# Issuing the stores of a memory-bound kernel from ScalarE's queue, loads from SyncE's

## Chip, cores, metric

The kernel runs on one core of a Trainium2 chip. The metric is the device time of one execution in microseconds (us). A profiled execution spans about 1.8 us less than its device time (81.2 of 83.02 us before). SP in the profile is SyncE, DVE is VectorE, ACT is ScalarE, and "SPq" and "ACTq" are their queues of transfers.

## The reference

```python
x = np.random.randn(1024, 4096).astype(np.float32)      # axis = -1
mean = np.mean(x, axis=axis, keepdims=True)
return ((x - mean) ** 2).astype(np.float32)
```

16.78 MB are read and 16.78 MB are written.

## The kernel before

The 1024 rows are two tiles of 128 partitions x 4 rows, so one partition's part of a tile is 64 KB in one piece. Both tiles have a buffer of their own, and all loads are issued at once. ScalarE computes the mean of row 3 and most of the squares, VectorE the other means and the last 1792 columns of row 2.

```python
Q = 4; HEAD = 512; H = D * 9 // 16
io = ctx.enter_context(tc.tile_pool(name="io", bufs=ntiles))      # ntiles = 2
for i in range(ntiles):
    x_tile = io.tile([P, Q * D], F32)
    cuts = [0, HEAD, Q * D] if i == 0 else [0, Q * D]
    for lo, hi in zip(cuts, cuts[1:]):
        nc.sync.dma_start(out=x_tile[:, lo:hi], in_=x_t[i][:, lo:hi])
    ...
for i in range(ntiles):
    row = [tiles[i][:, q * D:(q + 1) * D] for q in range(Q)]
    ...                                     # means, squares of rows 3, 0, 1
    square_on_act(row[2][:, :H], m2)
    back = row[2][:, H:]
    nc.vector.tensor_scalar_add(out=back, in0=back, scalar1=m2)
    nc.vector.tensor_mul(out=back, in0=back, in1=back)
    nc.sync.dma_start(out=out_t[i], in_=tiles[i])
```

Of the kernel before, what the change touches and what calls it, by code (L numbers as in the profile page):

```python
# [2 lines left out]

os.environ.setdefault("NEURON_RT_ULTRASERVER_MODE", "4")

# [4 lines left out]

F32 = mybir.dt.float32
ACT = mybir.ActivationFunctionType


@with_exitstack
def kernel(
    ctx: ExitStack,
    tc: tile.TileContext,
    x: bass.AP,
    axis: bass.AP,  # L20
    out: bass.AP,
):




    nc = tc.nc

    B, D = x.shape
    P = nc.NUM_PARTITIONS  # L30
    Q = 4
    HEAD = 512
    H = D * 9 // 16
    assert B % (P * Q) == 0
    ntiles = B // (P * Q)
    inv_d = 1.0 / float(D)

    x_t = x.rearrange("(n p q) d -> n p (q d)", p=P, q=Q)
    out_t = out.rearrange("(n p q) d -> n p (q d)", p=P, q=Q)

    io = ctx.enter_context(tc.tile_pool(name="io", bufs=ntiles))
    scratch = ctx.enter_context(tc.tile_pool(name="scratch", bufs=1))
    stats = ctx.enter_context(tc.tile_pool(name="stats", bufs=2 * ntiles * Q))

    tiles = []
# [5 lines that stand above are left out]
        tiles.append(x_tile)  # L51

    inorder = tc.keep_in_program_order

    def mean_on_act(row):
        copy = scratch.tile([P, D], F32)
        neg_mean = stats.tile([P, 1], F32)
        nc.scalar.activation(  # L58
            out=copy, in_=row, func=ACT.Identity, scale=-inv_d, accum_out=neg_mean
        )  # L60
        return neg_mean

    def mean_on_dve(row):
        neg_sum = stats.tile([P, 1], F32)
        neg_mean = stats.tile([P, 1], F32)
        inorder(nc.vector.reduce_sum(  # L66
            out=neg_sum, in_=row, axis=mybir.AxisListType.X, negate=True
        ))
        inorder(nc.vector.tensor_scalar_mul(out=neg_mean, in0=neg_sum, scalar1=inv_d))  # L69
        return neg_mean  # L70

    def square_on_act(part, neg_mean):
        inorder(nc.scalar.activation(  # L73
            out=part, in_=part, func=ACT.Square, bias=neg_mean, scale=1.0
        ))

    for i in range(ntiles):
        row = [tiles[i][:, q * D:(q + 1) * D] for q in range(Q)]
        m3 = mean_on_act(row[3])
        m0 = mean_on_dve(row[0])  # L80
        square_on_act(row[3], m3)
        m1 = mean_on_dve(row[1])
        square_on_act(row[0], m0)
        m2 = mean_on_dve(row[2])
        square_on_act(row[1], m1)
        square_on_act(row[2][:, :H], m2)
        back = row[2][:, H:]
        nc.vector.tensor_scalar_add(out=back, in0=back, scalar1=m2)  # L88
        nc.vector.tensor_mul(out=back, in0=back, in1=back)  # L89
        nc.sync.dma_start(out=out_t[i], in_=tiles[i])  # L90


# [1 line left out]
_INS = ['x', 'axis']  # L94
_OUTS = [((1024, 4096), 'float32')]

_NUMBERS = {'axis': -1}


# [26 lines left out]
```

## Time and profile before

| | before |
|---|---|
| time, median of 6 runs (range) | 83.06 us (83.00 to 83.20) |
| span of the profiled execution | 81.2 us |
| first store issued / second store issued | 39.42 / 58.70 us |
| last load packets end / first store's last packets end | 41.08 to 41.38 / 60.40 to 60.70 us |

A *packet* is here one record of one transfer engine: in these transfers one partition's row of a tile, 64 KB. A window of the profile (columns: window, width, busy time of DVE, ACT and POOL, clock, DMA share, GB/s) books a packet's whole time where the packet starts. So if a window holds the starts of exactly one packet for each of the 16 engines, its DMA share times its width is the mean duration of those packets. Three windows of the kernel before (columns: window, width, busy time of DVE, ACT and POOL, clock, DMA share, GB/s):

```profile
38.50:39.20 0.70, 0.70 (x1) 0.65 (x1) 0.00 (x0) 1.00 3.47 1498
...
41.00:41.80 0.80, 0.06 (x1) 0.06 (x1) 0.00 (x0) 1.00 3.03 1311
...
60.30:61.80 1.50, 0.00 (x0) 0.00 (x0) 0.00 (x0) 1.00 1.62 699
```

They hold the load's last packets (3.47 x 0.70 = 2.43 us), the first store's first packets (3.03 x 0.80 = 2.42 us) and the second store's first packets (1.62 x 1.50 = 2.43 us). All are alike. Going from the load to the store, and from the store to the next, costs an engine nothing here, on one queue: paired in order of time, each packet starts within 0.01 us of the end of the one before.

### The profile page before, as it was taken

How to read it: one execution, taken by the hardware profiler on the slowest of the kernel's cores; microseconds unless marked ns; L12 is line 12 of the kernel's file. 1: busy time of each engine (PE TensorE's matmuls, PEld its weight loads, DVE VectorE, ACT ScalarE, POOL GpSimd, SP SyncE). 2: the span in 40 equal slices, each digit the busy share in tenths (PEclk: the TensorE clock that was granted, in tenths of full speed). 3: DMA queues.
4: the chain of work that ended last, by engine and by line, in shares of the span. 5: the costliest groups of instructions: out<-in, count | busy, mean ns of one | idle time of the engine just before them, and what ended most of it. 6: DMA issues, size and time to landing. Idle time of an engine off the chain costs nothing.

```text
span 81.2 us, 83 instructions
## 1 busy us (share of the span) xinstructions
DVE 33.4 (41%) x16; ACT 34.7 (43%) x13; POOL 0.2 (0%) x4
## 2 busy tenths in 40 slices
DVE  0000000000099999999349999999800000000000
ACT  6000000000099999999249999999800000000000
POOL 0000000000000000000000000000000000000000
DMA  1999569999974999990999990999992899997490
GB/s 16 614 501 501 219 282 501 501 501 501 517 323 194 517 517 517 517 484 32 517 517 517 517 517 0 517 517 517 517 517 129 388 517 517 517 517 323 194 517 0
DMA packets 720, 33.55 MB, mean 413 GB/s; under 512 B 80, under 2 KB 80, under 8 KB 208
## 3 DMA queue, kind: packets, MB, share of 16 engines
q1 hardware_dynamic: 720, 33.55, 96.2%
HBM read 16.78 MB, written 16.78 MB: 413 GB/s over the span
## 4 chain that ended last, share of the span: by engine, by line
DMA 49%; DVE 21%; SPq 1%; issue 0%
DMA x_tile<-in_x_dram 49%; DVE neg_sum L66 16%; DVE x_tile L89 2%; DVE x_tile L88 1%; SPq L50 1%; DVE neg_mean L69 1%
## 5 line engine op out<-in xcount | busy, mean ns | idle before, releaser
L66 DVE TENSOR_REDUCE neg_sum<-x_tile 128x1 f32<-128x4096 f32 x6 | 26.5, 4413 | 24.9 <-DMA x_tile<-in_x_dram 24.9
L73 ACT ACTIVATE x_tile<-x_tile,neg_mean 128x4096 f32<-128x4096 f32 (+1 forms) x8 | 26.0, 3324 | 0.1
L58 ACT ACTIVATE copy<-x_tile 128x4096 f32<-128x4096 f32 x2 | 7.2, 3616 | 23.0 <-DMA x_tile<-in_x_dram 23.0
L89 DVE TENSOR_TENSOR x_tile<-x_tile 128x1792 f32<-128x1792 f32 x2 | 4.1, 2026 | 0.1
L88 DVE TENSOR_SCALAR x_tile<-x_tile,neg_mean 128x1792 f32<-128x1792 f32 x2 | 2.3, 1153 | 0.1
L58 ACT ACT_TABLE_LOAD x1 | 1.3, 1283 | 0.7 <-PEq L107 0.7
L69 DVE TENSOR_SCALAR neg_mean<-neg_sum 128x1 f32<-128x1 f32 x6 | 0.9, 154 | 0.2
L58 ACT ACTIVATION_READ_ACCUMULATOR copy<-x_tile 128x1 f32 x2 | 0.4, 186 | 0.0
L107 POOL MEMSET const-bfloat16-1.0<- 128x1 bf16 x1 | 0.1, 103 | 0.0
L107 POOL MEMSET const-uint8-127<- 128x1 uint8 x1 | 0.1, 103 | 0.0
L107 POOL MEMSET const-float32-1.0<- 128x1 f32 x1 | 0.1, 100 | 0.0
L107 POOL MEMSET const-float32-0.0<- 128x1 f32 x1 | 0.1, 99 | 0.2 <-issue 0.2
## 6 DMA issues: line engine op xcount, KB each, us to landing
x_tile<-in_x_dram SPq DMA_DIRECT2D x1, 7936.0 KB, 21.2
x_tile<-in_x_dram SPq DMA_DIRECT2D x1, 256.0 KB, 2.7
out_dram<-x_tile SPq DMA_DIRECT2D x2, 21.7
x_tile<-in_x_dram SPq DMA_DIRECT2D x1, 40.1
```

The source lines that it names most:

```text
L50: nc.sync.dma_start(out=x_tile[:, lo:hi], in_=x_t[i][:, lo:hi])
L58: nc.scalar.activation(out=copy, in_=row, func=ACT.Identity, scale=-inv_d, accum_out=neg_mean)
L66: inorder(nc.vector.reduce_sum(out=neg_sum, in_=row, axis=mybir.AxisListType.X, negate=True))
L69: inorder(nc.vector.tensor_scalar_mul(out=neg_mean, in0=neg_sum, scalar1=inv_d))
L73: inorder(nc.scalar.activation(out=part, in_=part, func=ACT.Square, bias=neg_mean, scale=1.0))
L88: nc.vector.tensor_scalar_add(out=back, in0=back, scalar1=m2)
L89: nc.vector.tensor_mul(out=back, in0=back, in1=back)
L107: nc = _bacc.Bacc("TRN2", target_bir_lowering=False, num_devices=1)
```

## The change

The intent is to give loads and stores separate queues, so that a store's wait for its data cannot hold up a load. In the kernel before, no load stands behind a store: SP's load issues end at 2.06 us, and its first store is issued at 39.42 us.

```diff
         nc.vector.tensor_mul(out=back, in0=back, in1=back)
-        nc.sync.dma_start(out=out_t[i], in_=tiles[i])
+        nc.scalar.dma_start(out=out_t[i], in_=tiles[i])
```

## The prediction

> **What bounds the kernel now.** I began with the busy shares, the slices and the queue of the page, because 33.55 MB pass through in about 80 us and the first question is whether the transfers leave room for anything else.
>
> ```profile
> DVE 33.4 (41%) x16; ACT 34.7 (43%) x13; POOL 0.2 (0%) x4
> ...
> DMA  1999569999974999990999990999992899997490
> GB/s 16 614 501 501 219 282 501 501 501 501 517 323 194 517 517 517 517 484 32 517 517 517 517 517 0 517 517 517 517 517 129 388 517 517 517 517 323 194 517 0
> ...
> q1 hardware_dynamic: 720, 33.55, 96.2%
> ```
>
> No compute engine is busy for half of the span, and the one DMA queue is busy for 96.2% of what 16 engines could give. The dips in the DMA row (a 0, a 2, a 4) look like holes. Whether they are holes decides this case, so I cut narrow windows about them; the last two columns are the DMA share and GB/s.
>
> ```profile
> 1.70:1.80 0.10, 0.00 (x0) 0.10 (x1) 0.00 (x0) 1.00 0.98 123
> ...
> 38.60:39.00 0.40, 0.40 (x1) 0.40 (x1) 0.00 (x0) 1.00 6.07 2621
> 39.00:41.00 2.00, 0.36 (x1) 0.15 (x1) 0.00 (x0) 1.00 0.00 0
> 41.00:41.40 0.40, 0.00 (x0) 0.00 (x0) 0.00 (x0) 1.00 6.07 2622
> ...
> 57.90:58.30 0.40, 0.40 (x1) 0.40 (x1) 0.00 (x0) 1.00 6.04 2621
> 58.30:60.30 2.00, 0.33 (x1) 0.20 (x1) 0.00 (x0) 1.00 0.00 0
> 60.30:60.80 0.50, 0.00 (x0) 0.00 (x0) 0.00 (x0) 1.00 4.85 2097
> ...
> 77.20:77.70 0.50, 0.00 (x0) 0.00 (x0) 0.00 (x0) 1.00 4.84 2097
> 77.70:79.60 1.90, 0.00 (x0) 0.00 (x0) 0.00 (x0) 1.00 0.00 0
> ```
>
> A share of 6.07 of 16 engines in 0.4 us is possible only if a packet's whole time is booked where it starts: 6.07 x 0.40 = 2.43 us and 4.85 x 0.50 = 2.42 us for each engine. So each engine starts one packet there that runs for 2.42 us, and the empty window after it is that packet in flight. The packet records agree: a tile's row of 65,536 bytes is one packet of 2.418 us, eight to an engine and transfer, and each starts within 0.02 us of the end of the one before. The dips are bookkeeping and there is no hole. 65,536 B / 2.418 us is 27.1 GB/s for one engine, 434 GB/s for 16, and 33.55 MB at that rate take 77.4 us. The first packets start at 1.75, the last ones at 77.2 to 77.7 and run until about 80.1: 78.3 us without a pause, of which 77.4 is bytes at full rate and 0.9 the start with its small first load. Before it lies 1.75 us of start, after it 1.1 us of landing and closing (span 81.2). The time of 83.02 is 1.8 us above the span, for what lies outside it.
>
> Then the timeline and SP's waits, to see what a later or earlier store would do.
>
> ```profile
> 37.33 2.03 DVE L89 TENSOR_TENSOR x_tile<-x_tile 128x1792 f32<-128x1792 f32 x1
> 39.42 19.62 SPq L90 DMA_DIRECT2D out_dram<-x_tile  x2
> 41.74 3.62 ACT L58 ACTIVATE copy<-x_tile 128x4096 f32<-128x4096 f32 x1 [2.59 <-DMA x_tile<-in_x_dram]
> ...
> 45.48 13.01 ACT L73 ACTIVATE x_tile<-x_tile,neg_mean 128x4096 f32<-128x4096 f32 x4
> ...
> 56.60 2.03 DVE L89 TENSOR_TENSOR x_tile<-x_tile 128x1792 f32<-128x1792 f32 x1
> ```
> ```profile
> SPq L90 <- DVE x_tile L89: 54.7, 2, 35.9
> SPq L121 <- DMA out_dram<-x_tile: 21.2, 2, 19.2
> ```
>
> SP is idle except for issuing: it waits for VectorE's last multiply before each store, then for the stores. No load stands behind a store on SP, since all three loads were issued by 2.1 us. The first store is issued at 39.42; the merged row gives the second at 39.42 + 19.62 - 0.34 = 58.70 (one issue is 0.34 to 0.35 us). From an issue to its first packet I take 1.0 us, from the first load (issued 0.73, first packet 1.75).
>
> So the first store is ready at 40.4, while the loads' last packets, started at 38.6 to 39.0, end at 41.0 to 41.4: it is early by 0.6 to 1.0 us. The second is ready at 59.7, while the first store's last packets, started at 57.9 to 58.3, end at 60.3 to 60.7: early by 0.6 to 1.0 us. The chain of waits gives 21% to VectorE and 49% to the load, but it is a chain through tile 1's computation with hardly any slack against the queue: the transfer queue is what sets the end.
>
> [...]
>
> **The change part by part.** The listing of both programs shows exactly one difference: two issues leave SP's end, and one stands on ScalarE after each tile's 2304-wide activation, with the same waits on ScalarE's and VectorE's semaphores. VectorE's order is the same.
> Removed: 2 x 0.345 = 0.69 us of SP, which is idle then; worth 0 on the path.
> Added: 2 x 0.345 us (SP's duration taken for ScalarE's) on ScalarE. The first sits in ScalarE's idle stretch: its square ends at about 39.15, VectorE at 39.36, so the issue runs from about 39.4 to 39.8, and the next activation waits for the load until 41.74. Margin 1.9 us, cost 0. The second comes after ScalarE's last activation (45.48 + 13.01 = 58.49), again after VectorE's end at 58.63. Cost 0.
> Moved: the issue itself by perhaps 0.05 us either way; it is early by 0.6 us, so 0.
> The store goes into another ring. The last load packets started at 38.6 to 39.0, before the store was even issued[...]. Cost 0.
> Sum: 0 us, 83.0 us.
>
> **The rivals.** (a) *The two rings share an engine more finely than by packets.* Then from 40.4 each engine gives the load's last 0.6 to 1.0 us half its rate, the load lands 0.6 to 1.0 us later, and tile 1's computation and the second store come as much later. The second store would be ready at 60.3 to 60.7, against a queue that is free at 60.3 to 60.7, since the bytes in total are the same. So a hole of 0 to 0.4 us: 83.0 to 83.4. Uniform packet times speak neither for nor against, as only one ring is in use. (b) *ScalarE's issue is slow*, in its first use of the queue above all. The margin of 0.6 to 1.0 us takes it up; only an issue 1.5 us slower would cost 0.5 to 0.9 us each, 84.0 to 84.8. Nothing in the profile speaks for it. (c) *Loads and stores on two rings overlap and go faster.* One row in flight already takes an engine at 27.1 GB/s, reading (63,488 bytes in 2.343 us) as writing (65,536 in 2.418), and no hole is left to fill. To gain 2%, 1.66 us, it would have to take more than the 0.9 us that the start loses, and no store is near the start. (d) *A second queue costs something outside the span or in the closing waits*: perhaps 0.1 to 0.3 us, no row can tell; 83.1 to 83.3.
>
> **Range and chances.** The best guess is 83.0. Below, only run scatter (83.0 to 83.2 before) and a slightly earlier issue: 82.7. Above, rivals (a) and (d) at 83.3 to 83.4 and scatter: 83.5. Two per cent is 1.66 us, that is over 84.7: only a slow issue at its worst, 3%. Faster by 2%, 1%. Within 2%, 96%.
>
> **What would show it.** Right: two queues in the queue view, the second with 16.8 MB and about half of the time, the sum near 96%; ScalarE's next activation still at 41.7; packets of 2.42 us with the first store's starting at 41.0 to 41.4 and the second's at 60.3 to 60.8; span 81.1 to 81.4. Rival (a): the load's last packets longer than 2.42 us, the activation at 42.3 to 42.7. Rival (b): a long issue on ScalarE, and a hole before a store. Rival (d): the same span and a longer time. The prediction is wrong if the span changes by more than 0.5 us, and wrong in its ground if that is without a hole in the queue.

The forecast's sum came to 0 us, 83.0 us: 0 each for the issues removed, for those added, for the one moved, and for the store's change of queue. The last 0 was an assumption. That two queues take turns packet by packet was seen only later, in head_act (0.08 and 2.34 us) and row3_early (0.61 and 2.42 us). The 0.1 to 0.3 us of rival (d) is a guess that no trace shows. A "ring" in this text and in the expectations is what the profile shows as a queue: q1, into which SP issues, and q10, into which ScalarE does.

## The result

The changed kernel takes 83.88 us (median of 6, 83.82 to 83.98) against 83.06. The ratio is 1.0096, with a 95% interval of 1.0083 to 1.0109. A ratio here is the mean time of one kernel's fast runs over that of the other's of the same rounds, so it is not quite the ratio of the medians. The change costs 0.8 us: within 2%, as predicted, but well clear of the noise and outside the predicted range of 82.7 to 83.5.

From the page of the changed kernel, first the busy shares, then the queues, then a line of the DMA issues:

```profile
DVE 33.4 (41%) x16; ACT 34.7 (42%) x13; POOL 0.2 (0%) x4
...
q10 hardware_dynamic: 288, 16.78, 48.1%
q1 hardware_dynamic: 432, 16.78, 48.0%
...
out_dram<-x_tile ACTq DMA_DIRECT2D x2, 22.5
```

The stores are now a queue of their own, q10. Together the queues are busy for 96.1% of a span that is 1.0 us longer, so there is no new hole: the packets themselves have become longer. A store now takes 22.5 us from issue to landing (median), 21.7 before. The timeline of the changed kernel:

```profile
37.50 2.03 DVE L89 TENSOR_TENSOR x_tile<-x_tile 128x1792 f32<-128x1792 f32 x1
39.61 0.38 ACTq L90 DMA_DIRECT2D out_dram<-x_tile  x1
41.91 3.62 ACT L58 ACTIVATE copy<-x_tile 128x4096 f32<-128x4096 f32 x1 [2.59 <-DMA x_tile<-in_x_dram]
...
56.77 2.03 DVE L89 TENSOR_TENSOR x_tile<-x_tile 128x1792 f32<-128x1792 f32 x1
58.88 0.34 ACTq L90 DMA_DIRECT2D out_dram<-x_tile  x1
```

Everything there is as before, 0.17 us later, since in this execution (the slowest of the six) the start of the loads was that much slower. ScalarE's issues take 0.38 and 0.34 us, and its next activation waits for the load, not for the issue. SP, which had waited for VectorE, now only waits at the end:

```profile
SPq L121 <- DMA x_tile<-in_x_dram: 39.8, 1, 39.8
SPq L121 <- DMA out_dram<-x_tile: 39.4, 2, 20.2
```

The windows that answer to the three of before:

```profile
38.50:39.20 0.70, 0.70 (x1) 0.70 (x1) 0.00 (x0) 1.00 3.46 1498
...
41.00:41.80 0.80, 0.00 (x0) 0.00 (x0) 0.00 (x0) 1.00 4.08 1311
...
60.30:61.80 1.50, 0.00 (x0) 0.00 (x0) 0.00 (x0) 1.00 1.62 699
```

The load's last packets are unchanged (3.46 x 0.70 = 2.42 us). The first store's first packets moved the same bytes but took 4.08 x 0.80 = 3.26 us, 0.84 us more than before. The second store, which follows on the same queue, starts with 2.43 us again. The packet records say the same: all 16 first packets are long, 3.09 to 3.47 us, and each begins within 0.01 us of the end of the engine's last load packet. That is the whole loss. In the mean over the engines the load ended 0.04 us later than before and the passage cost 0.84. The very last packet ends at 80.99 us in place of 80.02: the engine that ends last is the one whose first store packet was the longest (3.47 us, 1.05 too long), and its load had ended at 41.30 us, 0.08 before the latest engine of the kernel before.

### The profile page after: what moved, and what is told of

It is laid out like the page before. It is cut to its first block, busy times and chain, and to the rows that moved or that the text cites. A ratio compares the mean times of both kernels' runs of the same rounds, so it can differ in the third digit from the quotient of the medians.

```text
span 82.2 us, 82 instructions
## 1 busy us (share of the span) xinstructions
DVE 33.4 (41%) x16; ACT 34.7 (42%) x13; POOL 0.2 (0%) x4
## 4 chain that ended last, share of the span: by engine, by line
DMA 49%; DVE 20%; SPq 1%; issue 0%
DMA x_tile<-in_x_dram 49%; DVE neg_sum L66 16%; DVE x_tile L89 2%; DVE x_tile L88 1%; SPq L50 1%; DVE neg_mean L69 1%
## 6 DMA issues: line engine op xcount, KB each, us to landing
out_dram<-x_tile ACTq DMA_DIRECT2D x2, 22.5
```

## The experiments

Fourteen kernels were run. Edits are shown against the changed kernel, except where another is named. The times come from four executions of each kernel (row3_early: one), the packets from its one profiled execution. In what follows the *loss* is how much later an engine's first packet of the next transfer ends than it would if it followed the packet before at once and took 2.42 us, as the mean over the 16 engines. "Long" means over 2.8 us; in fact all long first packets took 2.89 us or more.

### Which queue, which store, which direction

**Queues swapped** (label swap): loads from ScalarE, stores from SP.

```diff
-            nc.sync.dma_start(out=x_tile[:, lo:hi], in_=x_t[i][:, lo:hi])
+            nc.scalar.dma_start(out=x_tile[:, lo:hi], in_=x_t[i][:, lo:hi])
-        nc.scalar.dma_start(out=out_t[i], in_=tiles[i])
+        nc.sync.dma_start(out=out_t[i], in_=tiles[i])
```

> Loads on ScalarE's queue, stores on SP's: the change turned round. In the changed kernel all 16 first packets of the first store take 3.09 to 3.39 us in place of 2.42, 0.83 us more. Theory S (a DMA engine that passes from one ring to the other loses about 0.83 us): the loss stays, now on SP's first store packets, time 0.8 over before, about 83.9. Theory F (the first big use of a ring loses it): the same here, 83.9. Theory A (ScalarE delivers its stores late or slowly): the loss is gone, 83.0 to 83.2, packets 2.42 us.

Measured: 83.97 us (83.86 to 84.42, 4 runs; ratio 1.0091). (The expectation gives the changed kernel's packets as 3.09 to 3.39 us; the trace has 3.09 to 3.47.) The time fits S and F, but the packets did not come out as either expected. Only 3 of 16 first packets were long, 3.09 to 3.25 us. The other 13 took 2.45 to 2.46 us, most of them starting about 0.2 us after the engine's last load packet. The mean loss was only 0.33 us. The end came late all the same in this execution, which was the slowest of the four (84.42 us), since one engine was behind in the loads (its last load packet ended at 42.13 us, before at 41.38 at the latest) and was one of the three long ones. So there are two modes, and this run alone does not tell what selects them.

**One store on each queue**, in both orders (labels store0_act, store1_act):

```diff
-        nc.scalar.dma_start(out=out_t[i], in_=tiles[i])
+        store_q = nc.scalar if i == 0 else nc.sync       # store0_act
+        store_q = nc.sync if i == 0 else nc.scalar       # store1_act
+        store_q.dma_start(out=out_t[i], in_=tiles[i])
```

> First store on ScalarE's queue, second back on SP's, so the engines pass from ring to ring twice. S: two losses, 1.6 to 1.7 over before, about 84.7, long first packets in both stores. F: one loss, on the first store alone, about 83.9, since SP's ring has been used by the loads. A: one loss, the first store's, 83.9.

> First store on SP's queue, second on ScalarE's: one passage, between two stores, with no turn from reading to writing at it. S, F and A: one loss of about 0.83 at the second store's first packets, about 83.9. Theory T (the loss needs the turn from loads to stores together with the change of ring): no loss, about 83.1.

Measured: store0_act 84.65 us (84.62 to 84.74, ratio 1.0164), store1_act 83.93 us (83.84 to 84.05, ratio 1.0077). The windows of store0_act:

```profile
41.00:41.80 0.80, 0.00 (x0) 0.00 (x0) 0.00 (x0) 1.00 4.09 1311
...
60.30:61.80 1.50, 0.00 (x0) 0.00 (x0) 0.00 (x0) 1.00 2.08 699
```

and of store1_act:

```profile
41.00:41.80 0.80, 0.00 (x0) 0.00 (x0) 0.00 (x0) 1.00 3.03 1311
...
60.30:61.80 1.50, 0.00 (x0) 0.00 (x0) 0.00 (x0) 1.00 2.19 699
```

In store0_act both stores begin long (4.09 x 0.80 = 3.27 us and 2.08 x 1.50 = 3.12 us), in store1_act only the second (2.19 x 1.50 = 3.28 us). So the loss comes once for each passage between the two queues. It is not ScalarE's doing (A falls: SP's second store is long too), not the first use of a queue (F falls: SP's had carried the loads), and it needs no turn from reading to writing (T falls: two stores in a row have it).

**The head load on ScalarE's queue** (label head_act):

```diff
+            load_q = nc.scalar if hi == HEAD else nc.sync
-            nc.sync.dma_start(out=x_tile[:, lo:hi], in_=x_t[i][:, lo:hi])
+            load_q.dma_start(out=x_tile[:, lo:hi], in_=x_t[i][:, lo:hi])
```

> As the changed kernel, but the small first load (256 KB) goes through ScalarE's queue as well, so that this ring has been used before the first store. S: the first store's first packets stay at 3.1 to 3.4 us, time 83.9 give or take what the start changes. F: they fall to 2.42 us, time about 83.1. A: they stay long.

Measured: 83.40 us (83.34 to 83.47, ratio 1.0013). No first packet was long; all took 2.45 to 2.47 us, most after a pause of about 0.15 us, a loss of 0.18 us. S as it stood expected them to stay long. The head's own small packets also took turns with the large ones of the other queue, and from the second large packet on each ran its ordinary 0.08 and 2.34 us. A passage as such is therefore free at times. In this kernel the store was issued at 39.87 us, 0.26 later than in the changed kernel, while the load ended at the same time. That suggested theory R, that the moment of issue decides.

### The moment of issue

**Later** (labels late03, late08, and late08_sp for the kernel before): VectorE multiplies N columns of its finished part of tile 0 by 1.0.

```diff
         nc.vector.tensor_mul(out=back, in0=back, in1=back)
+        if i == 0:
+            late = back[:, :N]             # N = 256, 1152, 1152
+            nc.vector.tensor_scalar_mul(out=late, in0=late, scalar1=1.0)
```

> The changed kernel with its first store issued some 0.34 us later (VectorE multiplies 256 columns of its part of tile 0 by 1.0, about 0.30 us and a start). So far two modes were seen at a change of ring: the store's packet starts at once and takes 0.7 to 1.0 us longer (long mode: the change, both one-store variants), or it starts 0.13 to 0.2 us after the load's last packet and takes 2.46 (short mode: the variant with the head load on ScalarE, and 13 of 16 engines with the queues swapped). Theory R: long mode is a packet that reaches its ring while the engine is still busy on the other ring; short mode one that finds the engine idle. R: most or all engines go to short mode, loss about 0.2 to 0.4, time 83.3 to 83.5, that is faster than the changed kernel although the store is later. Theory S (a first packet on another ring always costs 0.83): 83.9 to 84.2, packets stay above 3 us.

> The same with 1152 columns, some 0.84 us later. R: all 16 engines idle for 0.6 to 0.9 us before the store, then packets of 2.46 us; time 83.8 to 84.0, about that of the changed kernel. S: idle and loss add up, 84.5 to 84.8.

> Control: the kernel before with its first store as late as in the 0.84 us variant, on SP's own queue. R: idle as above, and no other cost, 83.7 to 84.0, the same as on ScalarE's queue within 0.15 us. S: the same here, so 0.8 us less than on ScalarE's queue.

Measured: late08 83.34 us (83.30 to 83.56, 4 runs as in all that follow, ratio 1.0037), late08_sp 83.44 us (83.41 to 83.51, ratio 1.0047), late03 83.93 us (83.75 to 84.04, ratio 1.0101). The added multiplies took 0.29 us in late03 and 0.76 us in the other two. The window of late08:

```profile
41.00:41.80 0.80, 0.03 (x1) 0.03 (x1) 0.00 (x0) 1.00 3.08 1311
```

Its first packets took 3.08 x 0.80 = 2.46 us, none was long, and most came after a pause of about 0.2 us. So a store issued 0.66 us *later* (40.27 in place of 39.61) made the kernel about 0.5 us *faster* (0.54 by the medians, 0.49 by the ratios). S, by which the loss comes at every passage, falls. The window of the control on SP's queue, late08_sp:

```profile
41.00:41.80 0.80, 0.00 (x0) 0.00 (x0) 0.00 (x0) 1.00 3.08 1311
```

It loses 0.25 us, like late08's 0.24: a store that comes this late costs the same on either queue. Both kernels idled less than I expected (0.6 to 0.9 us) and came in below the expected times. Nor does the pause look like a wait for a late issue, as theory R has it: ends and starts, paired in order of time, lie 0.18 to 0.24 us apart on every engine, although the ends are spread over 0.37 us in late08 and 0.55 us in late08_sp. The pause follows each engine's own end; its cause is not shown.

late03 hit the edge: 5 engines long, 11 short. R expected most or all to be short and a time of 83.3 to 83.5. The packets met the first, the time did not: the last engine to finish sets the time, and its first packet took 3.45 us, 1.03 too long. This execution (83.75 us) was also the fastest of the four. The median of 83.93 us alone would fit S.

**Earlier** (labels early06, head_early06, swap_early06): the changed kernel, head_act and swap, each with the first store some 0.8 to 1.3 us earlier. For tile 0 VectorE leaves out the subtraction and the columns are split anew. The result is wrong there; it still passed the comparison, because the means are near zero.

```diff
-        square_on_act(row[2][:, :H], m2)
-        back = row[2][:, H:]
-        nc.vector.tensor_scalar_add(out=back, in0=back, scalar1=m2)
+        cut = D - H if i == 0 else H
+        square_on_act(row[2][:, :cut], m2)
+        back = row[2][:, cut:]
+        if i > 0:
+            nc.vector.tensor_scalar_add(out=back, in0=back, scalar1=m2)
```

> The changed kernel with its first store issued about 0.6 us earlier (tile 0 leaves out the subtraction in VectorE's part and splits the rest anew; its result is wrong there on purpose). R, if earlier is in itself bad: long mode on all 16 engines, 83.8 to 84.1. If long mode is only a race near the load's end: short mode or no loss, 83.0 to 83.4.

> The variant with the head load on ScalarE's queue (short mode, 83.40), its first store 0.6 us earlier, wrong in the same place on purpose. R: now the store reaches its ring while all engines are well inside the load's last packet: long mode, first packets above 3 us, time 84.0 to 84.3. F2: stays short, 83.3 to 83.5.

> The variant with the queues swapped (13 of 16 engines short), its first store 0.6 us earlier, wrong in the same place on purpose. R: 14 to 16 engines in long mode, first packets' mean above 3 us in place of 2.59; time not below 84.0. If SP's ring as the taker is what made it short: the mean stays near 2.5.

**A queue used before** (label warm_act): the changed kernel with a useless 64 KB load on ScalarE's queue at the start.

```diff
+    warm = scratch.tile([P, 128], F32)
+    nc.scalar.dma_start(out=warm, in_=x_t[0][:, :128])
```

> The changed kernel, with a useless 64 KB load on ScalarE's queue at the very start, so that this ring has been used before the first store, as in the variant with the head load there, but with the other loads on SP as in the changed kernel. Question: was that variant in the short mode because its ring had been used, or because its store came at another moment? Theory F2 (a ring used before in the run is short): all first packets 2.46 us, time 83.2 to 83.5. Theory R (only the moment matters: the store's issue stands 1.4 to 1.9 us before the load's last packets end): long mode stays, 3.1 to 3.5 us, 83.9 to 84.1.

Measured: early06 84.03 us (84.03 to 84.05, ratio 1.0117), head_early06 84.03 (84.01 to 84.10, ratio 1.0118), swap_early06 84.13 (84.00 to 84.88, ratio 1.0147), warm_act 84.08 (84.03 to 84.15, ratio 1.0122). One line each, of head_act and of head_early06:

```profile
41.00:41.80 0.80, 0.00 (x0) 0.00 (x0) 0.00 (x0) 1.00 3.09 1311
```
```profile
41.00:41.80 0.80, 0.00 (x0) 0.00 (x0) 0.00 (x0) 1.00 4.08 1311
```

The kernel with the head load on ScalarE's queue goes from 2.47 to 3.26 us when its store comes 0.87 us earlier, and from 83.40 to 84.03. In all three early kernels all 16 first packets are long. In warm_act 14 of 16 are, so an earlier use of the queue does not help (F2 falls). All four go as R expected.

From the packet records of all these runs, worked out for each passage: the *margin* is the mean end of the engines' last packets of the transfer before, minus the start of the next transfer's issue.

| passage | margin, us | long first packets | loss, us |
|---|---|---|---|
| same queue: before, both stores | 1.82, 1.86 | 0 of 16 | 0.00 |
| same queue: changed kernel, second store | 2.56 | 0 of 16 | 0.00 |
| same queue: swap, second store; store1_act, first store | 1.51, 1.66 | 0 of 16 | 0.00 |
| same queue: late08_sp | 0.88 | 0 of 16 | 0.25 |
| other queue: late08 | 0.95 | 0 of 16 | 0.24 |
| other queue: swap | 1.19 | 3 of 16 | 0.33 |
| other queue: late03 | 1.35 | 5 of 16 | 0.44 |
| other queue: head_act | 1.39 | 0 of 16 | 0.18 |
| other queue: **changed kernel** | 1.67 | 16 of 16 | 0.84 |
| other queue: store0_act, store1_act, at the same kind of moment | 1.68, 1.68 | 16 of 16 | 0.85, 0.85 |
| other queue: warm_act | 1.70 | 14 of 16 | 0.72 |
| other queue: head_early06, early06, swap_early06 | 2.34, 2.54, 2.57 | 16 of 16 | 0.84 |
| other queue: store0_act, second store | 2.58 | 16 of 16 | 0.70 |

On one queue an early issue is free and a late one costs 0.25 us. On the other queue a late issue costs about the same, but an early one, which has to wait behind the packets of the queue in service, costs 0.7 to 0.85 us. How early it is makes little difference to the store's packets from 1.67 us on; but in the three early kernels the load's own last packets grew as well, by 0.04, 0.13 and 0.19 us in the mean (in the table's order). Between about 1.2 and 1.7 us both outcomes occur, and the mean margin alone does not sort them: late03 has five long packets at 1.35 us, head_act none at 1.39.

### In the midst of a transfer, and the size of the packets

**Row 3 stored early** (label row3_early; one look, state unknown):

```diff
         square_on_act(row[3], m3)
+        if i == 0:
+            nc.scalar.dma_start(out=out_t[i][:, 3 * D:], in_=row[3])
...
-        nc.scalar.dma_start(out=out_t[i], in_=tiles[i])
+        hi = 3 * D if i == 0 else Q * D
+        nc.scalar.dma_start(out=out_t[i][:, :hi], in_=tiles[i][:, :hi])
```

> The changed kernel with row 3 of tile 0 stored alone as soon as it is squared, at about 30 us, on ScalarE's queue, in the midst of the second load: 8 packets of 16 KB to an engine that take turns with load packets of 64 KB. The load lands about 8 x 0.60 = 4.8 us later, so the whole is slow, 87 to 89 us; what counts are the packets. S with a loss at each change of ring: each of some 16 changes costs 0.8 us, the load lands 15 us later. R: only the first store packet of each engine is long (0.60 + 0.8), the others 0.60 and 2.42, since both rings have work waiting from then on, as with the small packets of the head load that took turns with the large ones at no cost.

Measured: 85.46 us. Windows that each hold one load packet of every engine:

```profile
28.90:29.40 0.50, 0.50 (x1) 0.50 (x1) 0.00 (x0) 1.00 4.85 2097
31.30:31.80 0.50, 0.47 (x3) 0.50 (x1) 0.00 (x0) 1.00 5.28 2097
34.60:35.00 0.40, 0.40 (x1) 0.40 (x1) 0.00 (x0) 1.00 6.08 2621
37.60:38.10 0.50, 0.50 (x1) 0.50 (x2) 0.00 (x0) 1.00 4.84 2097
40.60:41.10 0.50, 0.00 (x0) 0.00 (x0) 0.00 (x0) 1.00 6.22 2097
```

The early store was issued at 29.91 us. The load packet that started after it took 5.28 x 0.50 = 2.64 us, 0.22 more than usual. Then 16 KB and 64 KB packets of the two queues took turns at 0.61 and 2.42 us, at no cost. The second store was issued at 39.84 us, with packets of both queues still waiting, and the load packet that started next took 6.22 x 0.50 = 3.11 us, 0.69 more. So S with a loss at every change falls again, and R was wrong on where the cost falls: not on the store's packet but on the load's. These windows fit a cost that comes when a new transfer reaches one queue while the other is well in service, rather than when the engine changes queue. The load landed only some 3.4 us later, not 4.8: only four of an engine's eight store packets came in between (2.4 us), and the two long load packets made up most of the rest (0.9 us). All this comes from a single execution.

**Smaller packets** (labels first_small, tail_small): the first store's first packets, or the load's last ones, cut to 16 KB.

```diff
-        nc.scalar.dma_start(out=out_t[i], in_=tiles[i])      # first_small
+        cuts = [(2 * D, 3 * D), (0, 2 * D), (3 * D, Q * D)] if i == 0 else [(0, Q * D)]
+        for lo, hi in cuts:
+            inorder(nc.scalar.dma_start(out=out_t[i][:, lo:hi], in_=tiles[i][:, lo:hi]))
-        cuts = [0, HEAD, Q * D] if i == 0 else [0, Q * D]    # tail_small
+        cuts = [0, HEAD, Q * D] if i == 0 else [0, 3 * D, Q * D]
```

> The changed kernel with tile 0 stored in three issues on ScalarE's queue, the first one row 2 alone, so that the first packet after the passage has 16 KB (0.605 us) in place of 64 KB; issued at the same moment, 39.6. Fixed cost: that packet takes about 1.4 us, loss 0.84, time 83.9 to 84.2. Share of the packet that takes over (0.84 of 2.42 is 35%): it takes about 0.82 us, loss 0.21, time 83.2 to 83.5.

> The changed kernel with the second load cut in two on SP's queue, the last part 16 KB rows, so that the last load packets have 16 KB in place of 64 KB. Fixed cost, or a share of the packet that takes over: loss near 0.84 in all, 83.8 to 84.2, perhaps spread over two packets if the store is taken before the load's last one. Share of the packet that leaves: loss near 0.21, 83.2 to 83.5.

Measured: first_small 84.01 us (83.91 to 84.08, ratio 1.0100), tail_small 83.33 us (83.12 to 83.38, ratio 1.0011, interval 0.998 to 1.004). The window of first_small with its first 16 KB store packets:

```profile
41.00:41.60 0.60, 0.00 (x0) 0.00 (x0) 0.00 (x0) 1.00 2.41 437
```

They took 2.41 x 0.60 = 1.45 us in place of 0.61: again 0.84 more. The loss is no share of the packet that takes over. In tail_small, where the load leaves in 16 KB packets, the first store packets took 2.42 us on 9 of 16 engines, 2.47 on two and 2.62 to 2.64 on five, and the loss was 0.08 us in the mean. The nine started at once and lost nothing, which no passage to the other queue did before. So small packets in the leaving transfer seem to take most of the loss away. But this store was also issued 0.23 us later than the changed kernel's, with a margin of 1.50 us, in the stretch where both outcomes occur. No run separates the two. A loss of 35% of the packet that leaves (0.84 of 2.42, so 0.21 of 0.61) fits five engines, but not the nine that lost nothing. What exactly is being waited for in the engine stays open.

first_small shows a side effect as well, in its timeline:

```profile
39.49 3.73 ACTq L92 DMA_DIRECT2D out_dram<-x_tile  x3
41.79 4.42 DVE L66 TENSOR_REDUCE neg_sum<-x_tile 128x1 f32<-128x4096 f32 x1 [2.39 <-DMA x_tile<-in_x_dram]
43.27 3.62 ACT L58 ACTIVATE copy<-x_tile 128x4096 f32<-128x4096 f32 x1 [4.07 <-issue]
```

Three issues in a row kept ScalarE's queue until 43.22 us. Its activation started 1.5 us after VectorE's work on the same tile, waiting for "issue" and not for data. The time does not show it (ratio 1.0100, the changed kernel's 1.0096), by my reading because the transfer engines were behind anyway; no run tests that.

No version beat the kernel before. The fastest with two queues, tail_small, head_act and late08, took 83.33 to 83.40 us.

## Why the prediction was wrong

- **What bounds the kernel** was right. The transfer engines run without a pause in both kernels (the queues are busy for 96.2% and 96.1% of the span), and the loss shows in the end of the last packets (80.99 us in place of 80.02).
- **Removed and added issues: 0 us** was right. ScalarE's issues took 0.38 and 0.34 us (0.345 assumed), and its next activation waited for the load.
- **Moved issues: 0 us** was right as far as it went: the first store was issued at 39.61 us in an execution that ran 0.17 us late as a whole, and was ready in time. The step took being early as safe on any queue. On the other queue it is what puts the store into the costly case, as late08 showed (a loss of 0.24 us with an issue 0.66 us later).
- **"The last load packets started at 38.6 to 39.0, before the store was even issued ... Cost 0."** This is the step that failed. The load's last packets did stay at 2.42 us. But that they were under way before the store's issue does not make the passage after them free. The step assumed that engines hand over between queues as smoothly as within one, which the trace before could not show with one queue in use. Passing to a transfer that waited on the other queue cost 0.84 us in the mean over the engines (first packets of 3.09 to 3.47 us in place of 2.42), and with it the sum of 0 us became 0.8 us. What an engine waits for in these 0.84 us stays open.
- **Rival (a)**, finer sharing, had the right place and the wrong effect: neither the load's packets nor its landing changed, and the loss was no hole. **Rival (b)**, a slow issue, and **rival (d)**, a cost outside the span, did not happen: the issues took 0.38 and 0.34 us, and the span grew by as much as the time (1.0 us in the profiled executions). **Rival (c)**, a gain from overlap, did not happen either, as predicted.
- **The test that the prediction set itself** worked: a span longer by over 0.5 us with no hole in the queue, so wrong in its ground.
- **Range.** The top of 83.5 came from (a) and (d) alone. No rival allowed for a cost of the handover itself, so the measured 83.88 had no place. The chance of 96% for "within 2%" held.

## What to carry to other kernels

When the transfer engines are already busy without a pause, keep loads and stores that follow one another on one queue: here the handover on one queue was free when the next transfer was waiting (a loss of 0.00 us), and a second queue had no hole to fill (the one queue was busy for 96.2% of the span). A second queue has to earn its cost, 0.84 us here for a transfer of 64 KB rows that waits behind the other queue (0.70 to 0.85 in the variants). In one run each, that fell to 0.08 us with smaller last packets (tail_small), to 0.18 with the head load on the stores' queue (head_act) and to 0.24 with an issue 0.66 us later (late08), but only to 0.44 with one 0.24 us later (late03). If the time moves and no engine shows a new hole, look at the durations of the packets where the queue changes.
